# In-place block sums, a second off-diagonal buffer, and norm work moved to GpSimd in a two-layer trunk

## The chip, the cores and the metric

One core of one Trainium2 chip runs the whole kernel in one launch. The metric is device time in microseconds (us), the median of timed runs. PE is TensorE (matmuls), PEld its weight loads, DVE VectorE, ACT ScalarE, POOL GpSimd; SP is the queue that issues most DMAs.

## The reference

Two layers run over 640 tokens: 128 context tokens and 512 latent tokens that share the weights. Each layer is an adaLN-modulated mixer (short conv, windowed attention, gated DeltaNet), an output projection with a gated residual, a second RMS norm with modulation, and a SwiGLU block. What the change touches is the last part, cut to its core:

```python
x  = x + g1 * y                                   # y: mixer output @ w_out
h2 = _rms(x, p['norm2_g']) * (1 + sc2) + sh2      # mean of squares over 1024 features
x  = x + g2 * ((jax.nn.silu(h2 @ p['w_gate']) * (h2 @ p['w_up'])) @ p['w_down'])
```

D_MODEL is 1024, D_FF 2816, everything float32.

## The kernel before

Activations are feature-major: xt[0..7] are tiles of 128 features by 640 tokens. Tokens are worked in two halves h of 320 columns (HB). For accuracy each float32 operand is split into a high part of type fp32r (a cast on ACT) and a low part (a subtraction, on DVE unless another engine is named); a product is three matmuls: high by high, high by low, low by high.

The order in which each engine gets its instructions is fixed at build time by a planner: it takes instructions in program order as their inputs and buffers come free in its own model of the time, and those under tc.high_priority() first. At run time each engine works through its own queue in order. A tile of a pool has a tag and a number of buffers; a new tile of that tag waits until one is free.

After the mixer, rows(LATE_OUT, ...) (line 1570, called at line 1611) computes the output projection. It loads w_out in four pieces of 256 columns (load_w, line 177: DMA to raw, high part line 172, low part line 173). The argument side names the pieces whose split goes to xhi/xlo, in pool fp; the others go to whi/wlo, in pool wp. Pool fp lies where the mixer's pool was, so its tiles can be written only when the mixer's tiles there are done. Products go in the order h, then m (the 128-row block). After each, residual (line 543, DVE) updates xt[m], and Norm.add (line 360) squares it on ACT and adds the square into acc on DVE (line 370), except for the last three m (two in the down projection), whose squares go straight to the sums.

Norm.stats (line 372) sums over features with one-column matmuls (lines 396, 398), raises the mean to the power -0.5 on GpSimd (line 403) and broadcasts the result with matmuls (line 406). PairNorm.half then makes, for each of eight feature blocks k, t1 (line 486, DVE), the value h2 (line 489, ACT) and its split (lines 476 and 477 in block, 172 and 173 in parts). For h = 0 these steps are handed back and interleaved with the products of h = 1; for h = 1 they run after the last product. The blocks of h2 are named b11, b21 (h = 0, feature blocks 0 to 3 and 4 to 7) and b12, b22 (h = 1). derive(j) builds the combinations nt1, t2, nt3, nt4 for each j.

The gate and up products of the first two 128-column blocks are done plainly (lines 1733 to 1735; sets: gate's weights in xhi/xlo, up's in whi/wlo). The others are done in pairs of blocks by class Pair, a seven-product scheme for 2x2 blocks (s1 to s7, 12 matmuls each) in place of eight. A Pair loads the diagonal weight blocks into D (tag raw, three buffers, shared with all other weight loads), the off-diagonal ones into O (tag rawx, one buffer), forms the sums Pa and Pb (tag ps, two buffers; lines 1648, 1651, 1652), and splits D into whi/wlo (d), Pa and Pb into xhi/xlo (a, b) and half of O into ohi/olo (o). Line 1669 copies the first bank negated to the next one (ACT); consume is Swiglu.gate (lines 1712, 1714) or Swiglu.up (line 1720 and a split). Between pairs, down adds chunks of the down projection to xt; at the end of layer 0 these rows feed the next layer's Norm in the same way. In layer 0, the adaLN products of layer 1 (lines 284 to 293) are spread among all of this.

Of the kernel before, what the change touches and what calls it, by code (L numbers as in the profile page):

```python
# [8 lines left out]
F32 = mybir.dt.float32  # L9
F32R = mybir.dt.float32r  # L10
# [39 lines left out]
XEV = 'VVVVVVVAVA'  # L50
LAG, LAST_V = 1, True
LATE_OUT = tuple(range(8))
# [56 lines left out]
def hybrid_trunk_kernel(  # L109
# [234 lines left out]
    class Norm:  # L344
# [15 lines left out]
        def add(self, k, parts=(0, 1)):  # L360

            if self.acc[0] is None or self.acc[1] is None and 1 in parts:
                for h in parts:
                    self.acc[h] = self.fp.tile([128, HH], F32, tag=f"acc{h}", name="acc", bufs=1)
                    A.activation(self.acc[h], self.xt[k][:, HB[h][0]:HB[h][1]], AF.Square)
                return
            for h in parts:
                sq = self.ft(HH, "sq")
                A.activation(sq, self.xt[k][:, HB[h][0]:HB[h][1]], AF.Square)
                V.tensor_tensor(out=self.acc[h], in0=self.acc[h], in1=sq, op=ALU.add)  # L370

# [37 lines left out]
        def half(self, h, k0=0, k1=KT_, later=False):  # L409

            n = HH
            if k0 not in self.a_:
                self.a_[k0] = self.a_fn(k0, k1)
            if self.bc[h] is None:
                with tc.high_priority() if HIS else ExitStack():
                    self.stats(h)
            segs = ((1, slice(0, 128)), (0, slice(128, n))) if h == 0 else ((0, slice(0, n)),)
            rests = []

            def step(i):  # L420
                if i < k1 - k0:
                    rests.append(self.high(k0 + i, h, segs, self.a_[k0][:, i]))
                if i >= LAG:
                    rests[i - LAG]()

            steps = [lambda i=i: step(i) for i in range(k1 - k0 + LAG)]
            if later:
                return steps
            for f in steps:
                f()  # L430
# [29 lines left out]
    class PairNorm(Norm):  # L460
# [18 lines left out]

        def value(self, k, h, dst):  # L480

            b0, b1 = HB[h]
            segs = ((1, slice(0, 128)), (0, slice(128, HH))) if h == 0 else ((0, slice(0, HH)),)
            t1 = self.ft(HH, "t1")
            for g, sl in segs:
                V.scalar_tensor_tensor(out=t1[:, sl], in0=self.xt[k][:, b0:b1][:, sl], scalar=self.a_[0][:, k, g:g + 1],
                                       in1=self.bc[h][:, sl], op0=ALU.mult, op1=ALU.mult)
            for g, sl in segs:
                A.activation(dst[:, sl], t1[:, sl], AF.Identity, bias=self.sh[:, k, g:g + 1])

        def half(self, h, later=False):
            if 0 not in self.a_:
                self.a_[0] = self.a_fn(0, KT_)
            self.stats(h)
            if h == 0:
                def step(i, j):
                    if i == 0:
                        self.first[j] = self.fp.tile([128, 2, HH], F32, tag="act", name="h0", bufs=8)
                    self.value(j + 4 * i, 0, self.first[j][:, i])
                    self.block(j, ("b11", "b21")[i], self.first[j][:, i], apool, G if j % 2 else V)  # L500

                return [lambda i=i, j=j: step(i, j) for i in range(2) for j in range(4)]
            room = [self.fp.tile([128, 3, HH], F32, tag=tag, name="h1", bufs=n) for tag, n in (("rawx", 1), ("ps", 2), ("ps", 2))]
            self.second = [room[(k + 1) // 3][:, (k + 1) % 3] for k in range(KT_)]
            for i in range(2):
                for j in range(4):
                    v = self.second[2 * j + i]
                    self.value(j + 4 * i, 1, v)
                    if i:
                        self.block(j, "b22", v, apool)  # L510
                    elif j < 2:
                        self.parts(j, "b12", v, *(self.fp.tile([128, HH], F32R, tag=tag, name=tag, bufs=2) for tag in ("ohi", "olo")))
                    else:
                        self.parts(j, "b12", v, *(self.fp.tile([128, HH], F32R, tag="tp", name="b12", bufs=TP_BUFS) for _ in range(2)))

        def parts(self, j, name, src, hi, lo):
            split(src, hi, lo)
            self.out[j][name] = (hi, lo)
# [1033 lines left out]
    for l in range(depth):  # L1552
# [5 lines left out]
        with tc.tile_pool(name=f"f{l + 1}", bufs=1, reuse_waits="tile") as fp:  # L1558
            last_layer = l == depth - 1
            fp.tile([128, 2, 4, 128], F32, tag="ps", name="ps", bufs=2)  # L1560
            fp.tile([128, 2, 4, 128], F32, tag="rawx", name="rawx", bufs=1)
            xt = [fp.tile([128, TOK], F32, name=f"xt{k}") for k in range(KT_)]
# [46 lines left out]
            for m in range(KT_):  # L1609
                nc.scalar.dma_start(out=xt[m], in_=xscr[m])  # L1610
            rows(LATE_OUT, w_out[l], 2, 4, mix[2:6], mods[l][:, 16:24], norm, side=(0, 1))
            seven = norm
# [12 lines left out]
            class Pair:  # L1625
# [8 lines left out]
                def __init__(self, w, f, consume):  # L1634
                    self.consume = consume
                    c0, c1 = f * 128, (f + 1) * 128
                    D = wp.tile([128, 2, 4, 128], F32, tag="raw", name="rawd", bufs=RAW_BUFS)
                    O = fp.tile([128, 2, 4, 128], F32, tag="rawx", name="rawo", bufs=1)
                    for dst, k0, c in ((D[:, 0], 0, c0), (D[:, 1], 4, c1), (O[:, 1], 0, c1), (O[:, 0], 4, c0)):
                        loads.append(nc.sync.dma_start(out=dst, in_=wslice(w, k0, 4, c, 128)))  # L1640
                    Pa, Pb = (fp.tile([128, 2, 4, 128], F32, tag="ps", name=name, bufs=2) for name in ("pa", "pb"))
                    self.d = [wp.tile([128, 2, 4, 128], F32R, tag=tag, name=tag, bufs=W_BUFS) for tag in ("whi", "wlo")]
# [3 lines left out]
                    with tc.high_priority():  # L1646
# [52 lines left out]
                def s7(self):  # L1699
                    self.product(Z, self.of(self.b, 1), "b22", False)  # L1700
                    self.consume(Z, 0, 1)

            class Swiglu:
# [12 lines left out]
                def up(self, src, i, h):  # L1716
# [113 lines left out]
```

## Time and profile before

| | |
|---|---|
| timed runs | 1804.47, 1806.52, 1807.45 us; median 1806.52 |
| profiled execution | 1814.66 us, span 1812.6 us |
| PE busy | 1701.5 us, 94% of the span |
| DVE busy | 1247.3 us, 69% |
| ACT busy | 782.1 us, 43% |
| POOL busy | 127.8 us, 7% |
| granted TensorE clock, mean | 0.965 |
| HBM traffic | 103 GB/s over the span |

Busy times count an engine's instructions, not its waits. The granted clock is in parts of full speed. Idle time of an engine matters only where the engine that sets the end waits for it. Layer 0's output projection starts near 417 us, its pairs run from about 495 to 900 us; layer 1's projection starts near 1304 us, its pairs run from about 1382 us to near the end.

### The profile page before, as it was taken

What the parts mean: (1) busy time and instruction counts of PE and PEld (TensorE: products, weight loads), DVE (VectorE), ACT (ScalarE), POOL (GpSimd) and SP (SyncE); (2) the same over time, 40 slices, a digit from 0 to 9 for tenths busy, and PEclk for the clock granted to TensorE, in tenths of its full rate; (3) what the DMA queues carried; (4) which work ended last, traced back from release to release, by engine and by line L of the source; (5) the groups of instructions that cost most, each with busy time, mean ns of one, the idle gap of its engine ahead of it and who ended that gap; (6) DMA issues with size and microseconds to landing.
All of it is one profiled execution on the core that took longest, in us unless ns stands there. A gap on an engine that the chain in (4) does not pass through costs nothing. (4 is left out here: it accounts for less than half of the span.)

```text
span 1812.6 us, 34382 instructions
## 1 busy us (share of the span) xinstructions
PE 1701.5 (94%) x13789; PEld 1512.9 (83%) x13789; DVE 1247.3 (69%) x2778; ACT 782.1 (43%) x1620; POOL 127.8 (7%) x242
## 2 busy tenths in 40 slices
PE   6998999999999999999999899899998999999998
PEld 3887875478889999999997889555897999999998
DVE  3799667665766767666677995686558766667664
ACT  3554234544543433433455532455345342534332
POOL 1110112100200000000012001120011000000000
PEclk7998998999999999999999989899989999999999
DMA  9512233654444222222131221445622322122312
GB/s 302 157 48 68 81 97 114 201 163 143 129 132 124 81 83 86 78 82 82 60 122 48 65 78 56 135 140 161 224 68 59 93 82 82 59 82 71 101 63 59
DMA packets 207693, 188.42 MB, mean 104 GB/s; under 512 B 12782, under 2 KB 182702, under 8 KB 207534
## 3 DMA queue, kind: packets, MB, share of 16 engines
q1 hardware_dynamic: 190656, 170.71, 30.8%
q10 hardware_dynamic: 16878, 15.53, 2.7%
q8 instruction: 108, 1.77, 0.4%
q14 instruction: 51, 0.42, 0.1%
HBM read 168.64 MB, written 17.56 MB: 103 GB/s over the span
## 5 line engine op out<-in xcount | busy, mean ns | idle before, releaser
L172 ACT CAST whi<-raw 128x1024 fp32r<-128x1024 f32 (+1 forms) x102 | 99.9, 980 | 111.7 <-PE pmm L201 34.9
L173 DVE TENSOR_TENSOR wlo<-raw,whi 128x1024 fp32r<-128x1024 f32 (+1 forms) x102 | 116.0, 1138 | 31.8 <-ACT whi L172 31.0
L202 PE MATMUL pmm<-hh,wlo 128*128 128x320 f32 x336 | 109.8, 328 | 6.2 <-DVE wlo L173 6.1
L199 PE MATMUL pmm<-hh,whi 128*128 128x320 f32 x336 | 110.2, 329 | 5.3 <-ACT dnp L614 3.7
L201 PE MATMUL pmm<-hl,whi 128*128 128x320 f32 x320 | 103.7, 324 | 0.0
L199 PE MATMUL pmx<-acth,whi 128*128 128x320 f32 x320 | 100.0, 313 | 3.9 <-DVE xt L543 3.8
L199 PE MATMUL pmm<-acth,whi 128*128 128x320 f32 x320 | 100.2, 313 | 1.4 <-DVE xt L543 1.4
L201 PE MATMUL pmx<-actl,whi 128*128 128x320 f32 x320 | 99.6, 311 | 0.0
L202 PE MATMUL pmx<-acth,wlo 128*128 128x320 f32 x320 | 99.4, 311 | 0.0
L202 PE MATMUL pmm<-acth,wlo 128*128 128x320 f32 x320 | 99.2, 310 | 0.0
L201 PE MATMUL pmm<-actl,whi 128*128 128x320 f32 x320 | 99.0, 309 | 0.0
L543 DVE SCALAR_TENSOR_TENSOR xt<-pmx,mod,xt 128x128 f32<-128x128 f32 (+2 forms) x168 | 68.9, 434 | 39.9 <-PE pmx L202 37.9
L543 DVE SCALAR_TENSOR_TENSOR xt<-pmm,mod,xt 128x128 f32<-128x128 f32 (+2 forms) x168 | 68.3, 432 | 29.4 <-PE pmm L202 18.7
L172 ACT CAST whi<-rawd 128x1024 fp32r<-128x1024 f32 x40 | 41.9, 1049 | 105.6 <-PE pmx L201 62.9
L173 DVE TENSOR_TENSOR xlo<-pb,xhi 128x1024 fp32r<-128x1024 f32 x40 | 49.0, 1225 | 38.0 <-ACT xhi L172 37.2
L199 PEld LDWEIGHTS pmm<-hh,whi 128*128 128x128 f32 x336 | 66.7, 199 | 7.5 <-ACT dnp L614 4.6
L202 PEld LDWEIGHTS pmm<-hh,wlo 128*128 128x128 f32 x336 | 66.3, 197 | 7.9 <-DVE wlo L173 7.0
L286 PE MATMUL pdn<-adaw,c 128*32 128x256 f32 x640 | 63.2, 395 | 9.3 <-DMA adaw<-in_ada_w_dram 9.3
L589 PE MATMUL pmm<-wlo,hh 128*128 128x256 f32 x240 | 69.2, 288 | 0.4 <-DVE wlo L173 0.4
L588 PE MATMUL pmm<-whi,hh 128*128 128x256 f32 x240 | 69.4, 290 | 0.0
L590 PE MATMUL pmm<-whi,hl 128*128 128x256 f32 x240 | 69.3, 289 | 0.0
L1648 DVE TENSOR_TENSOR pa<-rawd,rawo 128x1024 f32<-128x1024 f32 x40 | 50.2, 1255 | 25.4 <-DMA rawo<-in_w_gate_dram 13.4
(558 smaller groups left out, 5623.2 us busy)
## 6 DMA issues: line engine op xcount, KB each, us to landing
adaw<-in_ada_w_dram SPq DMA_DIRECT2D x80, 512.0 KB, 3.9
raw<-in_w_down_dram SPq DMA_DIRECT2D x44, 512.0 KB, 3.5
raw<-in_w_in_dram SPq DMA_DIRECT2D x36, 512.0 KB, 4.6
rawd<-in_w_gate_dram SPq DMA_DIRECT2D x40, 256.0 KB, 3.5
rawo<-in_w_gate_dram SPq DMA_DIRECT2D x40, 256.0 KB, 4.6
rawd<-in_w_up_dram SPq DMA_DIRECT2D x40, 256.0 KB, 3.4
rawo<-in_w_up_dram SPq DMA_DIRECT2D x40, 256.0 KB, 3.7
araw<-in_ada_w_dram SPq DMA_DIRECT2D x16, 512.0 KB, 5.7
```

Source lines behind the costliest of these rows:

```text
L172: (hi_eng or A.copy)(hi, src)
L173: (lo_eng or V).tensor_tensor(out=lo, in0=src, in1=hi.bitcast(F32), op=ALU.subtract)
L199: mm(o, lhsT=wh[:, k], rhs=ah, start=k == 0, stop=False)
L201: mm(o, lhsT=wh[:, k], rhs=al, start=False, stop=False)
L202: mm(o, lhsT=wl[:, k], rhs=ah, start=False, stop=not lead and k == n - 1)
L286: mm(pr[32 * q:32 * q + 32, 0:256], lhsT=c32[:, k], rhs=raw[:, q * 256:(q + 1) * 256], start=k == 0, stop=k == 7)
L543: V.scalar_tensor_tensor(out=x[:, sl], in0=pt[:, a0:a1], scalar=gate[:, g:g + 1], in1=x[:, sl], op0=ALU.mult, op1=ALU.add)
L588: mm(pt, lhsT=ah[:, ts], rhs=wh[:, k % 4], start=k == 0, stop=False)
L589: mm(pt, lhsT=ah[:, ts], rhs=wl[:, k % 4], start=False, stop=False)
L590: mm(pt, lhsT=al[:, ts], rhs=wh[:, k % 4], start=False, stop=k == 7)
L1648: V.tensor_tensor(out=flat(Pa), in0=flat(D), in1=flat(O)[:, 1:2].to_broadcast([128, 2, 512]), op=ALU.add)
```

## The change

- O (rawx) gets two buffers, ps one. The sums formerly in Pb are written over O: its second half becomes Pa[1] + D[0] and its first half O[0] + that sum. The two halves of b change places in s4 and s7.
- PairNorm's values are staged: t1 for step n is issued together with the value and split of step n - 2. The plain Norm keeps its lag of 1.
- For h = 1, PairNorm's stats runs under high priority.
- The adds of squares go to GpSimd, and so do the low parts of b12 for odd j.
- In the output projection the first two weight pieces go to whi/wlo and the last two to xhi/xlo, the other way round from before; the gate and up sets change places in the same way.
- The values of h = 1 lie in two rawx tiles and one ps tile instead of one and two.

```diff
-LAG, LAST_V = 1, True
+LAG, LAST_V = 2, True
...
-                V.tensor_tensor(out=self.acc[h], in0=self.acc[h], in1=sq, op=ALU.add)
+                G.tensor_tensor(out=self.acc[h], in0=self.acc[h], in1=sq, op=ALU.add)
...
-                if i >= LAG:
-                    rests[i - LAG]()
+                if i >= 1:
+                    rests[i - 1]()
...
+        def staged(self, h, order, rest):
+            ts = {}
+            def step(n):
+                if n < len(order):
+                    i, j = order[n]
+                    ts[n] = self.scaled(j + 4 * i, h)
+                if n >= LAG:
+                    i, j = order[n - LAG]
+                    rest(i, j, ts.pop(n - LAG))
+            return [lambda n=n: step(n) for n in range(len(order) + LAG)]
...
-            self.stats(h)
+            with tc.high_priority() if h else ExitStack():
+                self.stats(h)
...
-            room = [self.fp.tile([128, 3, HH], F32, tag=tag, name="h1", bufs=n) for tag, n in (("rawx", 1), ("ps", 2), ("ps", 2))]
+            room = [self.fp.tile([128, 3, HH], F32, tag=tag, name="h1", bufs=n) for tag, n in (("rawx", 2), ("ps", 1), ("rawx", 2))]
...
-            split(src, hi, lo)
+            split(src, hi, lo, lo_eng=G if j % 2 else V)
...
-            rows(LATE_OUT, w_out[l], 2, 4, mix[2:6], mods[l][:, 16:24], norm, side=(0, 1))
+            rows(LATE_OUT, w_out[l], 2, 4, mix[2:6], mods[l][:, 16:24], norm, side=(2, 3))
...
-                    O = fp.tile([128, 2, 4, 128], F32, tag="rawx", name="rawo", bufs=1)
+                    O = fp.tile([128, 2, 4, 128], F32, tag="rawx", name="rawo", bufs=2)
...
-                    Pa, Pb = (fp.tile([128, 2, 4, 128], F32, tag="ps", name=name, bufs=2) for name in ("pa", "pb"))
+                    Pa = fp.tile([128, 2, 4, 128], F32, tag="ps", name="pa", bufs=1)
...
-                        V.tensor_tensor(out=Pb[:, 0], in0=Pa[:, 1], in1=D[:, 0], op=ALU.add)
-                        V.tensor_tensor(out=Pb[:, 1], in0=Pb[:, 0], in1=O[:, 0], op=ALU.add)
-                        split(flat(Pb), flat(self.b[0]), flat(self.b[1]))
+                        V.tensor_tensor(out=O[:, 1], in0=Pa[:, 1], in1=D[:, 0], op=ALU.add)
+                        V.tensor_tensor(out=O[:, 0], in0=O[:, 0], in1=O[:, 1], op=ALU.add)
+                        split(flat(O), flat(self.b[0]), flat(self.b[1]))
...
-                    self.product(Y, self.of(self.b, 0), "t2", False)
+                    self.product(Y, self.of(self.b, 1), "t2", False)
...
-                    self.product(Z, self.of(self.b, 1), "b22", False)
+                    self.product(Z, self.of(self.b, 0), "b22", False)
...
-                    for w, use, side in ((w_gate, sw.gate, fp), (w_up, sw.up, None)) for i in range(2)]
+                    for w, use, side in ((w_gate, sw.gate, None), (w_up, sw.up, fp)) for i in range(2)]
```

## Rows read from the trace of the kernel before

**Rows 1.** Windows: stretch, length, busy (count) of PE, PEld, DVE, ACT, POOL, then PEclk.

```profile
440.00:530.00 90.00, 85.13 (x592) 75.49 (x592) 68.04 (x122) 48.49 (x103) 13.61 (x13) 0.96 0.43 130
530.00:900.00 370.00, 365.50 (x2458) 356.07 (x2457) 250.47 (x424) 145.88 (x241) 0.00 (x0) 1.00 0.29 86
1345.00:1420.00 75.00, 65.19 (x420) 61.84 (x419) 55.99 (x97) 38.88 (x83) 11.12 (x11) 0.95 0.21 64
1420.00:1760.00 340.00, 335.65 (x2241) 328.42 (x2240) 231.73 (x386) 132.51 (x217) 0.00 (x0) 1.00 0.26 78
```

**Rows 2.** TensorE's waits, 1345 to 1420 us: total us, times, longest.

```profile
PE pmm L1659 <- DVE av L1720: 2.8, 1, 2.8
PE pmm L1733 <- DVE sg L1714: 2.6, 1, 2.6
PE pkq L1659 <- ACT xhi L172: 1.2, 1, 1.2
...
PE pmm L1661 <- DVE wlo L173: 0.7, 1, 0.7
PE pkq L1745 <- DVE t L486: 0.6, 1, 0.6
```

**Rows 3.** Timeline of one pair's loads and split, layer 0: start, us, instruction.

```profile
668.61 1.23 DVE L173 TENSOR_TENSOR xlo<-pb,xhi 128x1024 fp32r<-128x1024 f32 x1 [0.45 <-ACT xhi L172]
...
670.87 0.69 DVE L1652 TENSOR_TENSOR pb<-pb,rawo 128x512 f32<-128x512 f32 x1
...
671.59 0.92 SPq L1640 DMA_DIRECT2D rawo<-in_w_gate_dram  x2
...
676.89 0.62 ACT L172 CAST ohi<-rawo 128x512 fp32r<-128x512 f32 x1 [1.04 <-DMA rawo<-in_w_gate_dram]
...
678.26 0.41 PE L1659 MATMUL pkq<-b,xhi 128*128 128x320 f32 x1 [0.86 <-ACT pkq L1669]
```

**Rows 4.** TensorE's waits over the whole span, one row.

```profile
PE pkq L1659 <- ACT pkq L1669: 4.9, 7, 1.3
```

**Rows 5.** Windows, second half of the second norm in layer 1.

```profile
1347.60:1354.60 7.00, 6.22 (x60) 5.95 (x59) 0.20 (x2) 1.24 (x4) 1.89 (x2) 1.00 0.01 2
1354.60:1365.50 10.90, 7.79 (x41) 7.29 (x40) 8.45 (x18) 8.03 (x19) 2.03 (x2) 0.83 0.00 0
1365.50:1390.20 24.70, 22.68 (x141) 22.07 (x142) 23.77 (x39) 12.33 (x25) 6.32 (x6) 0.94 0.22 64
```

**Rows 6.** Timeline, VectorE and TensorE, 1345 to 1354 us.

```profile
1345.72 0.55 DVE L543 SCALAR_TENSOR_TENSOR xt<-pmx,mod,xt 128x320 f32<-128x320 f32 x1
...
1353.45 1.12 PE L406 MATMUL pkq<-ident,ny 80*128 80x80 f32 x8 [0.78 <-POOL ny L403]
```

**Rows 7.** TensorE's waits, 500 to 530 us, layer 0.

```profile
PE pkq L1659 <- ACT pkq L1669: 1.2, 2, 0.8
PE pmx L1660 <- DVE nt L477: 1.0, 1, 1.0
```

**Rows 8.** Timeline, GpSimd and VectorE, 1335 to 1341 us.

```profile
1335.42 1.56 POOL L477 TENSOR_TENSOR b<-h,b 128x320 fp32r<-128x320 f32 x1 [10.57 <-ACT b L476]
...
1336.15 1.17 DVE L370 TENSOR_TENSOR acc<-acc,sq 128x320 f32<-128x320 f32 x1
...
1340.88 0.88 POOL L477 TENSOR_TENSOR b<-h,b 128x320 fp32r<-128x320 f32 x1 [3.91 <-ACT b L476]
```

**Rows 9.** Line 370 as a group: count, shortest, median and longest in ns.

```profile
L370 DVE TENSOR_TENSOR acc<-acc,sq x26: 477/483/1170, 429.8 to 1341.7; 128x320 f32<-128x320 f32 x26
```

**Rows 10.** Timeline, from the mixer into the output projection, layer 1.

```profile
1299.45 1.05 ACT L172 CAST whi<-raw 128x1024 fp32r<-128x1024 f32 x1 [2.83 <-DMA raw<-in_w_out_dram]
...
1301.03 0.65 PE L1392 MATMUL pmx<-pp,VS 128*64 128x256 f32 x4 [1.05 <-ACT pp L1390]
...
1302.79 1.05 ACT L172 CAST xhi<-raw 128x1024 fp32r<-128x1024 f32 x1
...
1312.90 0.68 DVE L543 SCALAR_TENSOR_TENSOR xt<-pmm,mod,xt 128x128 f32<-128x128 f32 x2 [3.16 <-DMA xt<-xscr]
```

More of the change, by code (lines that the diff above doesn't have):

```diff
@@ L422, in step @@
                     rests.append(self.high(k0 + i, h, segs, self.a_[k0][:, i]))
-                if i >= LAG:
-                    rests[i - LAG]()
-            steps = [lambda i=i: step(i) for i in range(k1 - k0 + LAG)]
+                if i >= 1:
+                    rests[i - 1]()
+            steps = [lambda i=i: step(i) for i in range(k1 - k0 + 1)]
             if later:
@@ L478, in block, with scaled, segs, value @@
             self.out[j][name] = (b[:, 0], b[:, 1])
-        def value(self, k, h, dst):
+        def scaled(self, k, h):
             b0, b1 = HB[h]
-            segs = ((1, slice(0, 128)), (0, slice(128, HH))) if h == 0 else ((0, slice(0, HH)),)
             t1 = self.ft(HH, "t1")
-            for g, sl in segs:
+            for g, sl in self.segs(h):
                 V.scalar_tensor_tensor(out=t1[:, sl], in0=self.xt[k][:, b0:b1][:, sl], scalar=self.a_[0][:, k, g:g + 1],
                                        in1=self.bc[h][:, sl], op0=ALU.mult, op1=ALU.mult)
-            for g, sl in segs:
-                A.activation(dst[:, sl], t1[:, sl], AF.Identity, bias=self.sh[:, k, g:g + 1])
+            return t1
+        def segs(self, h):
+            return ((1, slice(0, 128)), (0, slice(128, HH))) if h == 0 else ((0, slice(0, HH)),)
+        def value(self, k, h, t1, dst):
+            for g, sl in self.segs(h):
+                A.activation(dst[:, sl], t1[:, sl], AF.Identity, bias=self.sh[:, k, g:g + 1])
+        def staged(self, h, order, rest):
[8 more added lines that the diff above has]
+            return [lambda n=n: step(n) for n in range(len(order) + LAG)]
         def half(self, h, later=False):
@@ L493, in half, with rest @@
                 self.a_[0] = self.a_fn(0, KT_)
-            self.stats(h)
+            with tc.high_priority() if h else ExitStack():
+                self.stats(h)
+            order = [(i, j) for i in range(2) for j in range(4)]
             if h == 0:
-                def step(i, j):
+                def rest(i, j, t1):
                     if i == 0:
                         self.first[j] = self.fp.tile([128, 2, HH], F32, tag="act", name="h0", bufs=8)
-                    self.value(j + 4 * i, 0, self.first[j][:, i])
+                    self.value(j + 4 * i, 0, t1, self.first[j][:, i])
@@ L500, in step @@
                     self.block(j, ("b11", "b21")[i], self.first[j][:, i], apool, G if j % 2 else V)
-                return [lambda i=i, j=j: step(i, j) for i in range(2) for j in range(4)]
-            room = [self.fp.tile([128, 3, HH], F32, tag=tag, name="h1", bufs=n) for tag, n in (("rawx", 1), ("ps", 2), ("ps", 2))]
+                return self.staged(0, order, rest)
+            room = [self.fp.tile([128, 3, HH], F32, tag=tag, name="h1", bufs=n) for tag, n in (("rawx", 2), ("ps", 1), ("rawx", 2))]
@@ L504, in half, with rest @@
             self.second = [room[(k + 1) // 3][:, (k + 1) % 3] for k in range(KT_)]
[L505 to L514, printed above, removed]
+            def rest(i, j, t1):
+                v = self.second[2 * j + i]
+                self.value(j + 4 * i, 1, t1, v)
+                if i:
+                    self.block(j, "b22", v, apool)
+                elif j < 2:
+                    self.parts(j, "b12", v, *(self.fp.tile([128, HH], F32R, tag=tag, name=tag, bufs=2) for tag in ("ohi", "olo")))
+                else:
+                    self.parts(j, "b12", v, *(self.fp.tile([128, HH], F32R, tag="tp", name="b12", bufs=TP_BUFS) for _ in range(2)))
@@ L516, in parts @@
+            for f in self.staged(1, order, rest):
+                f()
         def parts(self, j, name, src, hi, lo):
-            split(src, hi, lo)
+            split(src, hi, lo, lo_eng=G if j % 2 else V)
             self.out[j][name] = (hi, lo)
@@ L1559, in hybrid_trunk_kernel @@
             last_layer = l == depth - 1
-            fp.tile([128, 2, 4, 128], F32, tag="ps", name="ps", bufs=2)
-            fp.tile([128, 2, 4, 128], F32, tag="rawx", name="rawx", bufs=1)
+            fp.tile([128, 2, 4, 128], F32, tag="ps", name="ps", bufs=1)
+            fp.tile([128, 2, 4, 128], F32, tag="rawx", name="rawx", bufs=2)
             xt = [fp.tile([128, TOK], F32, name=f"xt{k}") for k in range(KT_)]
```

## The prediction

> **What bounds the kernel now.** The first part of the page says which engine to follow: TensorE is busy for 94% of the span, VectorE for 69%, GpSimd hardly. No edit takes a matmul away, so the change can only win stretches in which TensorE waits or runs at the lower of its two clock levels. I then cut the span into the stages that the diff touches and read length minus PE busy in each [rows 1]. The two stretches of pairs, 530 to 900 and 1420 to 1760 us, leave 4.5 and 4.4 us of 710 at full clock: TensorE-bound, little to win. The stretch from the second norm to the first pairs leaves 4.9 us of 90 in layer 0 and 9.8 us of 75 in layer 1, where the granted clock is 0.95 as well. The waits of that stretch in layer 1 [rows 2] name VectorE first: 2.8 us for av, 2.6 us for sg. These two instructions are short; they are late because VectorE is busy 23.77 of the 24.7 us from 1365.5 on [rows 5]. So that stage is bound by the work queued on VectorE behind the norm's second half, and there most of the gain must come from.
>
> In the pairs I looked for the one wait that has to do with the off-diagonal loads, and followed it backwards [rows 3]: TensorE waits 0.86 us at 678.26 for the negated copy that ScalarE makes of the first bank; ScalarE was late because ohi, ahead of it in the same queue, sat 1.04 us until rawo landed; rawo was issued at 671.59, right behind line 1652 (670.87 to 671.56), the last reader of the one rawx buffer. All waits of that kind sum to 4.9 us in 7 places [rows 4], 1.2 us of it at 500 to 530 us [rows 7].
>
> **The change part by part.**
>
> *Sums in place, two rawx buffers.* Instruction count and shapes on every engine stay: line 1651 writes into O instead of Pb, line 1652 over O. The loads are the same four per pair. What moves is the release: before, the next O waits for line 1652; after, O is held until its sum is split (the xlo of b), but there is a second one, so the next load waits for the split of the pair before. In the trace that split ends at 668.61 + 1.23 = 669.84 and line 1652 at 671.56: the load gets only 1.7 us earlier, not a whole pair [rows 3]. That is more than the 1.04 us that ScalarE sat here, and the 1.3 us of the longest such wait [rows 4]. Outside 500 to 530 us there are 4.9 - 1.2 = 3.7 us to win; I take 2.5, because the load stands in SP's queue behind w_down's loads, which still wait for the raw buffers. Bounds 0 and 3.7. The single ps buffer costs nothing: Pa of the next pair is written on VectorE after the last reader of this one, on the same engine.
>
> *The norm's second half earlier and staged (layer 1).* Before, the last residual of the output projection runs on VectorE at 1345.72 to 1346.27, behind norm steps and square sums, and the broadcast of its statistics starts only at 1353.45 [rows 6]; from 1347.6 to 1354.6 VectorE does 0.20 us of work and ScalarE 1.24 [rows 5]. With priority the three late squares, the column sums on TensorE and the power on GpSimd come first: I estimate 3 of these 7 us saved. Then 1354.6 to 1365.5: VectorE busy 8.45 and ScalarE 8.03 of 10.9 us, so each waits for the other for 2.5 to 2.9 us; issuing the scaling two steps ahead takes most of that out, an estimate of 2 us. Together sg comes some 5 us sooner, more than the 2.6 us that TensorE waited for it. What goes with it: 2.6 + 0.6 us of waits [rows 2], and the low clock behind the gap, (1 - 0.94) x 24.7 = 1.5 us at the granted clock of 1365.5 to 1390.2 [rows 5]. Sum 4.7; bounds 0 and 4.7.
>
> *First pairs of layer 1.* They wait for 2.8 + 1.2 + 0.7 = 4.7 us [rows 2]. Late next is VectorE itself: TensorE now also arrives some 4.7 us sooner, while VectorE's queue starts 5 us sooner and has some idle taken out. The exchange of weight buffers lets the first pair's diagonal be split as soon as the gate's products end, not the up's. I take 3.0, bounds 0 and 4.7.
>
> *The same in layer 0.* There the adaLN products of the next layer fill TensorE, and sg costs it next to nothing. At 500 to 530 us it waits 1.2 us for the negated copy and 1.0 us for a low part of nt [rows 7]. I take 1.8, bounds 0 and 2.2.
>
> *Square sums and low parts on GpSimd.* 26 adds leave VectorE at 0.48 us each [rows 9], 12.5 us in all; two lows per layer (odd j) take 4 more. On GpSimd such an operation takes 0.88 us alone and 1.56 us where it meets VectorE; the add at 1336.15 took 1.17 us instead of 0.48 beside one [rows 8]. So a moved add frees 0.48 and, where it meets a two-input operation, costs up to 0.69. Between +0.48 and -0.21 us each, I take half: 26 x 0.13 = 3.5 us of VectorE time freed, all of it beside TensorE's work, and already inside the earlier residual above. The new cost is in GpSimd's queue: the power that every statistic needs can stand behind one add or one low. Bounds per statistic 0 and 1.56 us; on six statistics 0 to 9.4. I take 1.0 in all, since the trace shows GpSimd busy for some 2 us in stretches of 7 and 10.9 us here [rows 5].
>
> The Trainium skill (SBUF — State Buffer, Who interferes with whom) speaks against this part: a VectorE instruction with two SBUF inputs and a GpSimd instruction that reads SBUF lock each other out for the whole instruction. The pair at 1335.42 and 1336.15 agrees; the median of 483 ns beside a maximum of 1170 [rows 9] says that most of these adds met nobody. By the rule taken at its worst, all 30 moved operations would block VectorE for 0.88 us, 26 us against 14 freed.
>
> *Exchange of buffers at the output projection.* Before, its first weights go into xhi, which overlays the mixer's tiles: the split comes at 1302.79, while the weights for the later columns were split at 1299.45 into whi; TensorE meanwhile waited 1.05 us inside the attention's tail [rows 10]. After, the first products can fill such gaps. But the residual that frees the bank waits for xt, 3.16 us at 1312.90 [rows 10], and xt isn't moved: what TensorE wins in front it may stand for behind. I take 1.0 per layer, bounds 0 and 2.0, together 2.0.
>
> **Sum.** 2.5 + 4.7 + 3.0 + 1.8 + 2.0 - 1.0 = 13.0 us. The profiled execution's own time is 1814.66 us (span 1812.6 and 2.1 around it), which would become 1801.7. The median of the timed runs is 1806.52, 8.1 us below the profiled one; the same 13.0 off it gives 1793.5 us. The ends: all bounds won, 3.7 + 4.7 + 4.7 + 2.2 + 4.0 = 19.3, and some idle that I can't name, 3 us: 1784. Nothing won and the queue at its worst: 1816.
>
> **The rivals.**
>
> *Covered.* VectorE is the bound of the stage, and what the norm gains is spent in the weight splits behind it; in the output projection xt decides. Only the O loads and a little remain: -2.5 - 1.0 + 0.5, 1803.5 us. For it: 23.77 of 24.7 us busy. Against it: the 2.5 to 2.9 us of mutual waiting in front.
>
> *GpSimd's queue decides: slower.* Adds and lows stand ahead of the power at 1.56 us each, six times, 9.4 us, with TensorE standing directly for it (it already waits 0.78 us for the power at 1353.45 [rows 6]); the four b12 lows come 1.56 - 0.48 = 1.1 us later each on the chain of the second half, 4.3 us. The norm's gain is gone; O loads and buffers keep 4.5: +9.2, 1815.7 us. It decides from where GpSimd's queue holds the power longer than the 3 us that priority gains. The lock rule cited above would drive it. Against it: GpSimd is idle most of these stages.
>
> *All of it.* Every listed stall goes: 1784 to 1787 us.
>
> *The change doesn't do what it says.* SP's queue keeps O behind w_down's loads, and the second buffer changes nothing: 1793.5 + 2.5 = 1796 us.
>
> **How the numbers follow.** Forecast 0.46, covered 0.21, slower 0.15, all 0.13, O unchanged 0.05. A change under 0.2% (3.6 us) can't be told from none here. Faster: 0.46 + 0.13 + 0.05 and a third of covered, 0.71. Same: the rest of covered and a little of the slower case, 0.16. Slower 0.13. The range 1784 to 1808 leaves out most of the slower case and the far end of the best. For the forecast alone it is 1789 to 1799.
>
> **What would show it.** Right: between the two norm halves of layer 1 VectorE's gap shrinks from 7 to about 4 us; the wait of line 1733's first matmul for sg is gone, and the first pair follows some 5 us sooner; ohi's waits for rawo shrink, and TensorE's waits for the negated copy fall below 2 us; output-projection matmuls stand between the last attention products. Wrong: the power starts late behind an add on GpSimd, the stretch 1345 to 1420 keeps its length, or new waits for xt stand in the projection. Anything that moves the mixers by more than a few us would have a cause that I haven't named.

## The result, and the profile after

The changed kernel takes 1784.54 us (median of 4 runs, 1783.57 to 1785.53) against 1805.49 us for the kernel before (4 runs, too): ratio 0.989, 95% interval [0.9865, 0.9915]. That is 21 us faster; 13 were forecast. The profiled executions took 1783.57 us (span 1781.6) and 1814.66 us. The kernel before, profiled once more, took 1801.69, so 31 us between the first two profiles overstates the change.

Below the norm every line stands 25 lower now (L543 is L568, L1659 is L1684, L1669 is L1694, L1714 is L1739, L1720 is L1745, L1733 is L1758), in the experiments 24 to 27. The busy times over the span after:

```profile
span 1781.6 us, 34378 instructions
PE 1685.3 (95%) x13789; PEld 1506.5 (85%) x13789; DVE 1233.8 (69%) x2748; ACT 782.3 (44%) x1620; POOL 160.1 (9%) x272
```

Span less PE busy is TensorE's idle time: 96.3 us, before 1812.6 - 1701.5 = 111.1. The same by stage: I cut the span at the last attention product, the last broadcast of the norm's statistics, the first and the last pair, and the first product of layer 1. Windows of the kernel before, columns as in [rows 1]: output projection, second norm and pairs of layer 1, and, last, the end of layer 0 (down products and the next norm).

```profile
1303.20:1354.30 51.10, 47.97 (x333) 46.04 (x329) 27.59 (x62) 21.71 (x48) 6.22 (x6) 0.93 0.40 124
1354.30:1381.20 26.90, 23.69 (x141) 23.19 (x141) 24.15 (x43) 16.39 (x37) 8.35 (x8) 0.87 0.07 20
1381.20:1776.00 394.80, 384.79 (x2556) 374.71 (x2556) 270.06 (x448) 157.82 (x262) 0.00 (x0) 1.00 0.26 78
893.50:945.90 52.40, 50.34 (x343) 48.98 (x342) 37.70 (x87) 26.82 (x58) 8.53 (x15) 0.93 0.31 100
```

The same four of the kernel after:

```profile
1280.40:1328.00 47.60, 42.94 (x297) 41.01 (x294) 24.11 (x54) 21.90 (x48) 15.12 (x14) 0.93 0.39 123
1328.00:1352.80 24.80, 24.80 (x161) 24.80 (x161) 23.62 (x39) 15.78 (x36) 11.53 (x10) 0.93 0.08 22
1352.80:1745.00 392.20, 386.13 (x2556) 377.84 (x2556) 270.48 (x451) 158.38 (x265) 0.00 (x0) 0.99 0.26 79
881.10:932.70 51.60, 50.33 (x343) 49.13 (x343) 33.62 (x77) 26.90 (x59) 17.84 (x25) 0.93 0.31 99
```

Three things are to be seen in layer 1. The projection's window holds 36 matmuls fewer (333 to 297), an effect of the exchanged weight buffers to a large part: 16 stand ahead of it now, inside the attention's tail (the mixer in front has 3399, before 3383), and 20 behind the last broadcast (141 to 161). VectorE has 8 instructions fewer there, and 10 fewer at the end of layer 0; GpSimd has them (6 to 14, 15 to 25): the adds of squares. And the norm stage has no idle time left (3.2 us before), while the projection has more (3.1 to 4.7). With both profiles of each kernel, idle time in us:

| stage | before, twice | after, twice | mean change |
|---|---|---|---|
| two mixers | 77.6, 79.6 | 72.0, 70.4 | -7.4 |
| two output projections | 5.3, 4.4 | 8.9, 8.5 | +3.8 |
| two second norms | 3.5, 3.0 | 0.0, 0.0 | -3.2 |
| two stretches of pairs | 18.2, 15.1 | 9.6, 11.1 | -6.3 |
| end of layer 0 | 2.1, 2.2 | 1.3, 1.3 | -0.9 |
| tail | 4.6, 4.6 | 4.5, 4.6 | 0.0 |
| whole span | 111.1, 108.8 | 96.3, 95.8 | -13.9 |

Half of the fall is in the mixers, where only the exchange of buffers moves instructions. Since the matmuls that the exchange moves to the front fill idle time there and are missing in the projection, the two rows belong together: 83.4 to 79.9 us, or -3.6. The norms and the pairs fell by 9.5.

The rest of the 21 us is the busy time of the same 13789 matmuls: 1701.5 and 1691.1 before, 1685.3 and 1684.4 after.

TensorE's waits in the kernel after, 1350 to 1745 us, answer to [rows 2]:

```profile
PE pkq L1684 <- ACT pkq L1694: 2.8, 1, 2.8
PE pmm L199 <- DVE xt L568: 2.7, 1, 2.7
PE pkq L1684 <- ACT u L1710: 0.2, 1, 0.2
PE pmm L1686 <- DVE wlo L173: 0.2, 1, 0.2
```

The waits for av and sg are gone. The two at the top are new in size (in the first profile before, the longest of their kinds are 1.3 and 1.1 us); the second stands once in layer 0 as well, 2.7 us at 830.87. Ahead of this stretch, 1270 to 1365 us, the kernel after waits in other places, too:

```profile
PE pkq L406 <- POOL ny L403: 1.6, 2, 0.8
PE pmm L199 <- DVE xt L568: 1.4, 1, 1.4
PE pxo L396 <- POOL acc L370: 1.2, 1, 1.2
```

The second half of the norm in layer 1, timeline and windows of the kernel after, answers to [rows 5, 6]:

```profile
1321.23 0.54 DVE L568 SCALAR_TENSOR_TENSOR xt<-pmx,mod,xt 128x320 f32<-128x320 f32 x1
1321.70 1.19 ACT L391 ACTIVATE sq<-xt 128x320 f32<-128x320 f32 x3
...
1325.89 0.16 DVE L401 TENSOR_SCALAR nms<-pxo 80x4 f32<-80x4 f32 x1 [3.14 <-PE pxo L398]
1326.13 1.02 POOL L403 TENSOR_TENSOR ny<-nms,mhalf 80x4 f32<-80x4 f32 x1 [4.08 <-DVE nms L401]
...
1327.20 1.12 PE L406 MATMUL pkq<-ident,ny 80*128 80x80 f32 x8 [0.79 <-POOL ny L403]
1328.41 0.55 DVE L485 SCALAR_TENSOR_TENSOR t<-xt,msc,pkq 128x320 f32<-128x320 f32 x1 [2.36 <-PE pkq L406]
```

```profile
1321.70:1328.40 6.70, 5.91 (x57) 5.64 (x56) 1.21 (x5) 2.29 (x7) 2.20 (x3) 0.99 0.27 78
1328.40:1352.80 24.40, 24.40 (x158) 24.40 (x157) 23.62 (x39) 15.78 (x36) 11.53 (x10) 0.93 0.08 23
```

From the last residual to the broadcast it is 5.97 us (1321.23 to 1327.20), before 7.73 (1345.72 to 1353.45): 1.8 us sooner. Behind it VectorE is busy for 23.62 of 24.4 us, and TensorE never stands.

### The profile page after: what moved, and what is told of

The parts are those of the page before. It is cut to its first block, busy times and chain, and to the rows that moved or that the text cites. A ratio compares the mean times of both kernels' runs of the same rounds, so it can differ in the third digit from the quotient of the medians.

```text
span 1781.6 us, 34378 instructions
## 1 busy us (share of the span) xinstructions
PE 1685.3 (95%) x13789; PEld 1506.5 (85%) x13789; DVE 1233.8 (69%) x2748; ACT 782.3 (44%) x1620; POOL 160.1 (9%) x272
## 5 line engine op out<-in xcount | busy, mean ns | idle before, releaser
L568 DVE SCALAR_TENSOR_TENSOR xt<-pmx,mod,xt 128x128 f32<-128x128 f32 (+2 forms) x168 | 69.0, 434 | 50.2 <-PE pmx L202 47.9
L202 PE MATMUL pmx<-acth,wlo 128*128 128x320 f32 x320 | 99.8, 312 | 0.0
L201 PE MATMUL pmm<-actl,whi 128*128 128x320 f32 x320 | 99.8, 312 | 0.0
L568 DVE SCALAR_TENSOR_TENSOR xt<-pmm,mod,xt 128x128 f32<-128x128 f32 (+2 forms) x168 | 68.4, 433 | 38.1 <-PE pmm L202 25.8
L370 POOL TENSOR_TENSOR acc<-acc,sq 128x320 f32<-128x320 f32 x26 | 28.6, 1101 | 615.9 <-ACT sq L369 615.4
L173 DVE TENSOR_TENSOR xlo<-rawo,xhi 128x1024 fp32r<-128x1024 f32 x40 | 49.0, 1225 | 27.4 <-ACT xhi L172 26.5
```

The lines of the kernel that those rows point to most:

```text
L173: (lo_eng or V).tensor_tensor(out=lo, in0=src, in1=hi.bitcast(F32), op=ALU.subtract)
L201: mm(o, lhsT=wh[:, k], rhs=al, start=False, stop=False)
L202: mm(o, lhsT=wl[:, k], rhs=ah, start=False, stop=not lead and k == n - 1)
L568: V.scalar_tensor_tensor(out=x[:, sl], in0=pt[:, a0:a1], scalar=gate[:, g:g + 1], in1=x[:, sl], op0=ALU.mult, op1=ALU.add)
```

## The experiments

All ratios are to the kernel before. Idle time is span less PE busy of one profile. The two repeats set what either can tell: 2.3 and 0.5 us of idle time, and a few per mille of the timed runs. The last column but one is the idle time outside the mixers, to be set against 33.6 us in the first profile before and 24.3 in the first after; it varies by 4.3 and 1.1 us between the repeats. It leaves out the mixers, where only the exchange moves instructions, and so it serves to compare kernels that have the same weight buffers.

| kernel | timed us | ratio, 95% interval | idle | outside the mixers | PE busy |
|---|---|---|---|---|---|
| e1, without the O buffers | 1786.03 | 0.9909 [0.9879, 0.9938] | 96.6 | 27.1 | 1686.6 |
| e2, without the exchange | 1789.04 | 0.9924 [0.9896, 0.9953] | 95.5 | 22.0 | 1689.0 |
| e3, without GpSimd's part | 1794.42 | 0.9944 [0.9924, 0.9964] | 101.8 | 30.0 | 1685.5 |
| e4, without staging and priority | 1790.57 | 0.992 [0.9904, 0.9936] | 101.1 | 29.2 | 1689.7 |
| e5, before again | 1806.53 | 0.9986 [0.9961, 1.0011] | 108.8 | 29.2 | 1691.1 |
| e6, after again | 1786.11 | 0.988 [0.984, 0.9921] | 95.8 | 25.4 | 1684.4 |
| e7, GpSimd's part alone | 1794.54 | 0.9941 [0.9906, 0.9976] | 103.3 | 26.2 | 1687.7 |
| e8, staging and priority alone | 1797.28 | 0.9936 [0.9911, 0.996] | 107.4 | 25.0 | 1695.7 |
| e9, adds back on VectorE | 1797.7 | 0.9942 [0.9918, 0.9966] | 99.8 | 27.4 | 1691.5 |
| e10, O buffers alone | 1805.81 | 1.0003 [0.9974, 1.0031] | 109.3 | 30.0 | 1698.0 |
| e11, residuals and negated copies first | 1782.31 | 0.9859 [0.983, 0.9889] | 92.8 | 19.1 | 1688.3 |
| e12, gates' small steps first, too | 1781.62 | 0.9879 [0.9846, 0.9912] | 97.1 | 20.3 | 1682.7 |

### One part undone

**e1**, the sums and buffers of the pairs as before:

```diff
-                    O = fp.tile([128, 2, 4, 128], F32, tag="rawx", name="rawo", bufs=2)
+                    O = fp.tile([128, 2, 4, 128], F32, tag="rawx", name="rawo", bufs=1)
...
-                        V.tensor_tensor(out=O[:, 1], in0=Pa[:, 1], in1=D[:, 0], op=ALU.add)
+                        V.tensor_tensor(out=Pb[:, 0], in0=Pa[:, 1], in1=D[:, 0], op=ALU.add)
```

> The changed kernel with one rawx buffer, two ps buffers and Pb again; all else as changed. Theory A (the norm's second half and the first pairs behind it carry the gain, the O loads 2.5 us): about 1787.5 us, with 1805.5 for before and 1784.5 for the changed kernel. Theory B (the pairs carry it: O loads come early enough to take ScalarE's waits away everywhere): 1790 us or more, and TensorE's waits for the negated copy back near 4.9 us.

Timed, nothing can be told from the changed kernel, which speaks against theory B; B's sign, the waits for the negated copy, came back all the same. The waits over the whole span of e1 say why that costs little:

```profile
PE pkq L1684 <- ACT pkq L1694: 6.6, 7, 1.6
PE pmm L199 <- DVE xt L568: 3.6, 6, 1.3
```

The waits for negated copies are back, but the two of 2.7 us for xt in the down products are gone. e10 shows the other side.

**e2**, the weight buffers of the projection as before:

```diff
-            rows(LATE_OUT, w_out[l], 2, 4, mix[2:6], mods[l][:, 16:24], norm, side=(2, 3))
+            rows(LATE_OUT, w_out[l], 2, 4, mix[2:6], mods[l][:, 16:24], norm, side=(0, 1))
...
-                    for w, use, side in ((w_gate, sw.gate, None), (w_up, sw.up, fp)) for i in range(2)]
+                    for w, use, side in ((w_gate, sw.gate, fp), (w_up, sw.up, None)) for i in range(2)]
```

> The changed kernel with the buffer sides of the output projection and of the gate and up sets as before. Theory A: the gaps in the attention's tail come back, 2 us in all, 1786.5 us. Rival (the loads of xt decide, so what TensorE wins in front it waits for behind): 1784.5 us within 1. If the side also decides when the first pair can start: 1790 us.

Against the mean of the two profiles after, idle time grows by 2.3 us in the mixers (71.2 to 73.5) and shrinks by 2.9 in the projections (8.7 to 5.8): what TensorE wins in front it stands for behind, as the rival says. Timed it is 0.0034 slower than the changed kernel, nearer to the 1790 us of the last theory, but the intervals overlap; unclear.

**e3**, adds and low parts back on VectorE:

```diff
-                G.tensor_tensor(out=self.acc[h], in0=self.acc[h], in1=sq, op=ALU.add)
+                V.tensor_tensor(out=self.acc[h], in0=self.acc[h], in1=sq, op=ALU.add)
...
-            split(src, hi, lo, lo_eng=G if j % 2 else V)
+            split(src, hi, lo)
```

> The changed kernel with the adds of squares and the low parts of b12 back on VectorE. Theory A: VectorE's relief lies beside TensorE and GpSimd's queue costs about 1 us: 1783.5 to 1785.5 us. Rival 1 (GpSimd's queue holds the statistics): undoing it wins, 1780 us or less. Rival 2 (the freed VectorE time is what brings the second half forward): 1788 us or more.

Rival 2 holds, 1788 or more: ratio 0.9944 [0.9924, 0.9964], the only one of the four above the changed kernel's interval; idle time +5.7. Its interval overlaps with that of e4, so which of these two parts is worth more is not told by undoing them. TensorE's waits of e3, 1350 to 1745 us, show some of it: av and xhi (and sg, 0.3 us) stand ahead of the first pairs again.

```profile
PE pkq L1684 <- ACT pkq L1694: 3.0, 1, 3.0
PE pmm L199 <- DVE xt L568: 2.7, 1, 2.7
PE pmm L1684 <- DVE av L1745: 1.5, 1, 1.5
PE pmx L1684 <- ACT xhi L172: 0.7, 1, 0.7
```

The end of layer 0 in e3, the window to set against the fourth row after, has its 10 adds and nearly 1 us of idle time back (2.22 against 1.27):

```profile
883.50:936.70 53.20, 50.98 (x343) 48.99 (x342) 37.33 (x87) 26.84 (x58) 8.55 (x15) 0.94 0.30 97
```

In every profile with the adds on VectorE this idle time is 2.1 to 2.3 us; with the adds on GpSimd it is 1.3 (1.8 in e11 and e12, which order the residuals otherwise).

**e4**, lag and priority as before (the lag of 1 that the change replaces was the plain Norm's; PairNorm had none):

```diff
-LAG, LAST_V = 2, True
+LAG, LAST_V = 0, True
...
-            with tc.high_priority() if h else ExitStack():
-                self.stats(h)
+            self.stats(h)
```

> The changed kernel without the lag of 2 in PairNorm and without the priority of the second statistics. Theory A: the wait of line 1758 (1733 before) for sg and the low clock behind it come back and the first pairs start late again: 1792 to 1794 us. Theory B (the pairs carry the gain): 1788 us or less.

Between the theories: idle time +5.1, ratio 0.992, its interval overlaps with the changed kernel's. The gate's wait for sg comes back with 0.5 us only, not 2.6 [rows 2], so GpSimd's part goes a long way to take it away alone; in layer 0 the first pair waits 1.5 us for av.

### Repeats, and parts alone

**e5** and **e6** are the two kernels again, without an edit.

> The kernel before, unchanged, for a second profile. Both theories: the stages that the change touches (both projections to the next mixer) take the same 1038.7 us within 1.5, since their instruction order is fixed. If the mixers (416.6 and 357.3 us in the first profile) are as long again, the changed kernel's shorter mixers (409.9 and 347.7 us with the same order of matmuls) are an effect of the change; if they fall to about 411 and 350 us, the first profile was a long execution and the change didn't touch them.

> The changed kernel, unchanged, for a second profile: 1784.5 us within 5, its touched stages 1024.0 us within 1.5. This is the yardstick for what a difference between two profiles is worth.

The repeats agree less well than expected: the touched stages take 1035.4 us in e5 and 1020.0 in e6, 3.3 and 4.0 less than in the first profiles. The mixers take 414.6 and 349.9 us in e5, so the first was no shorter to speak of and the second 7.4: the first profile was a long one there, and mixer lengths of two single profiles don't show an effect of the change. Much of such a difference is the clock. The end of layer 0 in e6, against the fourth row after:

```profile
887.20:935.70 48.50, 47.25 (x344) 46.04 (x343) 33.55 (x77) 26.81 (x59) 17.81 (x25) 1.00 0.33 106
```

Same kernel, same matmuls, 1.25 against 1.27 us of idle time: 3.1 us shorter at a granted clock of 1.00 instead of 0.93. This is why I went over to idle time.

**e7** is the kernel before with e3's lines in their new form, **e8** the kernel before with e4's, made from the changed kernel by undoing the rest:

```diff
 # e7: undone beside e1 and e2
-LAG, LAST_V = 2, True
+LAG, LAST_V = 0, True
...
 # e8: undone beside e1 and e2
-                G.tensor_tensor(out=self.acc[h], in0=self.acc[h], in1=sq, op=ALU.add)
+                V.tensor_tensor(out=self.acc[h], in0=self.acc[h], in1=sq, op=ALU.add)
```

> The kernel before with only the adds of squares and the b12 lows moved to GpSimd. After the runs that undid one part, theory C: the time that this frees on VectorE is what brings the second half of the norm forward, so it wins much by itself, touched stages 1031 us or less, 1796 us. Theory A (prediction): nothing or 1 us lost, 1804 to 1806 us.

> The kernel before with only the staging by two steps and the priority of the second statistics. Theory A: 9.5 us won, 1796 us, touched stages 1029 us. Theory C (VectorE's queue still holds the last residuals and so the squares, whatever their priority): 3 us or less won, touched stages 1036 us or more.

Timed both are near 0.994, some 11 us each: theory C in e7 and theory A in e8, whose touched stages, 1028.5 and 1031.5 us, lie on the same side. By the whole idle time GpSimd's part alone takes 6.7 us off (mean before 110.0) and staging 2.6, but that difference is no effect of the parts. It is all in the first mixer, where neither edit touches a line; e7, then e8:

```profile
0.00:413.90 413.90, 366.05 (x3667) 284.76 (x3667) 288.10 (x809) 190.84 (x457) 49.04 (x111) 0.94 0.44 138
0.00:418.20 418.20, 366.10 (x3665) 285.61 (x3667) 287.80 (x809) 190.38 (x457) 49.01 (x111) 0.93 0.43 136
```

That is 47.9 against 52.1 us of idle time. Outside the mixers staging takes 6.4 off the mean before of 31.4, GpSimd's part 5.2: the two parts can't be told apart in size. They differ in what they end. e7 still waits 0.9 us for sg and 2.7 for av in layer 1, e8 for neither. And from the last residual of layer 1's projection to the broadcast it is 7.70 us in e7 (1324.48 to 1332.18) and in e4 (1325.73 to 1333.43), as before the change, but 6.16 in e8 (1339.41 to 1345.57) and 6.15 in e3 (1327.37 to 1333.52): this chain is shorter where the statistics have priority, and GpSimd's adds make no difference to it.

### Which half of GpSimd's part, and the O buffers alone

**e9**, only the adds back on VectorE:

```diff
-                G.tensor_tensor(out=self.acc[h], in0=self.acc[h], in1=sq, op=ALU.add)
+                V.tensor_tensor(out=self.acc[h], in0=self.acc[h], in1=sq, op=ALU.add)
```

> The changed kernel with the 26 adds of the squares back on VectorE; the low parts of second-half blocks stay on GpSimd (two of four per layer). Undoing both together cost about 8 us of the touched stages (1032.4 against 1024.0 and 1020.0) and came to 1794.4 timed. Theory 'adds': the 26 adds hold nearly all of it, since they are what VectorE had between the residuals that the attention projection's last products wait for: 1792 to 1795, touched stages 1028 to 1032, attention-to-gate stages of both layers 4 us longer each, and the wait of the statistics (L396) for acc goes. Theory 'lows': the few low parts lie right between the second half's values and the first pairs, and they hold most: 1784 to 1788, touched stages about 1022. My own first reading, that GpSimd's queue costs 1 us: 1783 to 1785, with the 1.17 us waits at the statistics gone in both layers.

Theory "adds": 0.9942 like e3, idle time +3.8 of its +5.7. The four lows are left with the difference, 1.9, no more than a repeat varies. The sign that this theory named, an end of the wait for acc, did not come: the statistics' first products wait in either kernel. Whole span, e9 and then the kernel after:

```profile
PE pxo L396 <- DVE acc L370: 4.4, 5, 1.6
```

```profile
PE pxo L396 <- POOL acc L370: 2.3, 2, 1.2
```

On VectorE an add takes half as long and still is awaited longer. In e9's timeline its square is ready on ScalarE by 1319.07, and it stands behind a weight split:

```profile
1318.25 0.82 ACT L369 ACTIVATE sq<-xt 128x320 f32<-128x320 f32 x2
1318.38 1.23 DVE L173 TENSOR_TENSOR wlo<-raw,whi 128x1024 fp32r<-128x1024 f32 x1 [0.21 <-ACT whi L172]
1319.52 0.49 DVE L370 TENSOR_TENSOR acc<-acc,sq 128x320 f32<-128x320 f32 x1
```

**e10**, the kernel before with the O buffers alone (e2, e3 and e4 undone together):

```diff
-LAG, LAST_V = 2, True
+LAG, LAST_V = 0, True
...
-            split(src, hi, lo, lo_eng=G if j % 2 else V)
+            split(src, hi, lo)
```

> The kernel before with only the two buffers for off-diagonal loads and the sums in place. Theory 'separate': the buffers are worth what undoing them cost, 1.8 us of touched stages, near the 2.5 us forecast: 1801 to 1805 beside a before of about 1805, touched stages 1034 to 1036 against 1037. Theory 'needs the rest': the off-diagonal halves matter only when the second half no longer sets the start of the first pairs, so alone they give nothing: 1805 +- 1.5, and ohi's wait for rawo shrinks without the first pair starting earlier. Theory 'steady pairs': the two buffers also help pairs outside the first: pairs0 and pairs1 each at least 2 us shorter than 397.7 and 393.8.

Theory "needs the rest" has the number: 1.0003 [0.9974, 1.0031], idle time -0.7, touched stages 1036.9 us; the steady pairs got no 2 us shorter each (400.1 and 393.3). But the reason is another than that theory's. Its waits for negated copies are gone (4.9 us in 7 places before, 2.9 in 6 in e5), and this row of the whole span is there instead:

```profile
PE pmm L199 <- DVE xt L567: 5.6, 3, 2.7
```

Two waits of 2.7 us for xt stand in every kernel with the second rawx buffer but e11 and e12, and in none without. The kernel after at the first of them:

```profile
828.18 0.34 DVE L568 SCALAR_TENSOR_TENSOR xt<-pmm,mod,xt 128x128 f32<-128x128 f32 x1
828.44 0.68 DVE L1677 TENSOR_TENSOR rawo<-rawo 128x512 f32<-128x512 f32 x1
829.16 1.23 DVE L173 TENSOR_TENSOR xlo<-rawo,xhi 128x1024 fp32r<-128x1024 f32 x1
830.31 0.41 DVE L568 SCALAR_TENSOR_TENSOR xt<-pmm,mod,xt 128x192 f32<-128x192 f32 x1
...
830.87 0.39 PE L199 MATMUL pmm<-acth,whi 128*128 128x320 f32 x1 [2.67 <-DVE xt L568]
```

A residual is two instructions here. Between them VectorE takes the second sum and its split, which have priority, and TensorE waits for the bank that the residual frees.

### A version that takes the new waits away

In the first pair of layer 1 it is ScalarE's order; the kernel after:

```profile
1355.30 0.68 DVE L1677 TENSOR_TENSOR rawo<-rawo 128x512 f32<-128x512 f32 x1
...
1356.07 1.05 ACT L172 CAST xhi<-rawo 128x1024 fp32r<-128x1024 f32 x1 [2.00 <-DVE rawo L1677]
1357.02 0.42 ACT L1694 ACTIVATE pkq<-pmm 128x320 f32<-128x320 f32 x1
...
1357.49 0.42 PE L1684 MATMUL pkq<-t,xhi 128*128 128x320 f32 x1 [2.82 <-ACT pkq L1694]
```

The negated copy stands behind a split that waited 2.00 us for the in-place sum. **e11** puts residuals and negated copies ahead:

```diff
-                    residual(xt[m], pt, h, gate[:, m])
+                    with tc.high_priority():
+                        residual(xt[m], pt, h, gate[:, m])
...
-                    A.activation(Y, self.x, AF.Copy, scale=-1.0)
+                    with tc.high_priority():
+                        A.activation(Y, self.x, AF.Copy, scale=-1.0)
```

> The changed kernel with two more steps put ahead in the planner's order: the residual of the projection and of the feed-forward down products, and the negated copy that the first pair's second product adds to. They aim at what the changed kernel's trace now names: TensorE waits for xt in down products 7.4 us over 4, for the negated copies 3.6 us over 2, for xt in the projection 2.1 us over 2. Theory 'waits go': 6 to 10 us less than the changed kernel, 1775 to 1780. Theory 'turned into other waits': what stood ahead on VectorE, the splits of the next weights, is now late instead; TensorE then waits for xlo or wlo about as long, 1783 to 1787. Theory 'worse': weight splits that were hidden become the bound in every chunk of down products, over 1788.

Between "waits go" and "turned into other waits". Both waits of 2.7 us for xt are gone, the negated copy is down to 0.6 us in either layer; what stands there instead, 1350 to 1745 us:

```profile
PE pmx L1685 <- DVE sg L1741: 2.7, 1, 2.7
PE pmm L1687 <- DVE wlo L173: 0.7, 2, 0.5
PE pkq L1685 <- ACT pkq L1696: 0.6, 1, 0.6
```

Idle time 92.8, the lowest here (19.1 outside the mixers against 24.3 and 25.4), ratio 0.9859 [0.983, 0.9889]. It beats the kernel before; against the changed kernel the intervals overlap, and the two were not timed in the same rounds.

**e12** puts the gates' small steps ahead, too:

```diff
-                    use(o, i, h)
+                    with tc.high_priority():
+                        use(o, i, h)
```

> The kernel with residuals and negated copies first, and beside them the gates' own small operations on VectorE and ScalarE (the sg and av steps of the first set of feed-forward products) put ahead in the planner's order, against the 2.7 us for which the first pair of layer 1 waited for sg in that kernel. TensorE's idle time over the span was 96.3 and 95.8 us in the changed kernel, 92.8 with residuals first; the busy time of its 13789 matmuls differs by up to 10 us between profiles of one kernel with the granted clock, so idle time is the measure. Theory 'the wait goes': idle 89.5 to 91, 1778 to 1781 timed. Theory 'it moves again': the splits of the first pair's weights come later and TensorE waits for xhi or xlo instead: idle 92 to 95, 1781 to 1785.

"It moves again". The wait for sg is gone, and 1270 to 1745 us has these, near the first pairs:

```profile
PE pkq L1685 <- ACT pkq L1696: 2.1, 2, 1.5
PE pmx L1686 <- DVE nt L477: 1.8, 1, 1.8
...
PE pmx L1685 <- ACT xhi L172: 0.9, 1, 0.9
```

The whole idle time, 97.1 us, lies above the ranges of both theories, since the mixers, which the edit does not touch, have 76.8 of it. Outside the mixers it is 20.3 us, in e11 19.1, so e12 wins nothing.

## Why the prediction was right and wrong

The direction and the bound (VectorE's queue from the second norm to the first pairs) were right. The time was not well hit: 1784.5 lies half a microsecond inside the lower edge of the stated range, 9 us below the forecast of 1793.5 and outside its 1789 to 1799. It is a time of the rival "all of it", but not by that rival's way: not every listed stall went, and new ones came. Idle time fell by 13.9 us where 13.0 less the 1.5 of clock were forecast. By stage that is near as well: norms and pairs 9.5, forecast (4.7 - 1.5) + 3.0 + 1.8 + 2.5 - 1.0 = 9.5; mixers with projections 3.6, forecast 2.0. By part it is not, so that the sums agree is in part luck: the O buffers gave less than forecast, GpSimd's part more. The step that failed is the term of -1.0, which had the wrong sign.

*GpSimd's part.* I put 26 x 0.13 = 3.5 us of VectorE time down as "beside TensorE's work", and 1.0 us as a loss in GpSimd's queue. Measured, it is a gain as large as the staging's: 5.7 us of idle time when undone, 5.2 alone outside the mixers, some 10 us timed either way. I priced collisions at half of the worst case. VectorE's busy time fell by 1247.3 - 1233.8 = 13.5 us, from e3 to the kernel after by 1245.4 - 1233.8 = 11.6, and the moved operations are worth 26 x 0.483 + 4 x 0.48 = 14.5, so by these sums collisions cost VectorE some 1 to 3 us in all, 0.1 per moved operation at most. The Trainium skill's lock rule (SBUF — State Buffer, Who interferes with whom), which I weighed against this part, agrees with the spread of GpSimd's adds, 868 ns at the least and 1855 at the most, median 880:

```profile
L370 POOL TENSOR_TENSOR acc<-acc,sq x26: 868/880/1855, 418.6 to 1315.1; 128x320 f32<-128x320 f32 x26
```

Its worst case, 26 us, did not come about: 18 of the 26 adds took less than 1 us. And the freed time was not "beside": VectorE had no slack behind the norm ([rows 5], 23.77 of 24.7 us), so the 3.5 us of adds in a projection (VectorE's busy time there, 27.59 to 24.11) can come out of all that is queued behind them. That the gain comes this way is argued; what e7 and e4 show is that it isn't a shorter chain from the last residual to the broadcast (7.70 us in both, 7.73 before). The queue's cost, up to 9.4 us in the slower rival, isn't there. The statistics wait 1.2 us once per layer for acc, 2.3 in all, but this wait is 0.4 us in e7, and with the adds on VectorE and all else as changed it is longer, 4.4 us in e9 and 5.3 in e3. The power's wait stayed (0.78 to 0.79 us at the second half, 5.9 to 5.4 over the span).

*Staging and priority, first pairs, layer 0* (4.7 + 3.0 + 1.8). The mechanism was right: the waits for sg and av are gone. The size is uncertain, 2.6 us of idle time alone (6.4 outside the mixers), undone 5.1; 8.0 were forecast without the clock. GpSimd's part works on the same waits: the gate's for sg, 2.6 us before, is 0.9 us in e7 and 0.5 in e4, and not there at all with staging, alone (e8) or with both. VectorE's gap didn't shrink from 7 to 4 us as I said (6.7 us with 1.21 of work in it, before 7.0 with 0.20 [rows 5]); the chain got 1.8 us shorter, 1.6 of it in e8, and the norm stage 2.5 (two profiles each: 26.9 and 27.2 to 24.8 and 24.3), where I had the first pair 5 us sooner.

*O buffers* (2.5). The waits for the negated copy went as read from [rows 3, 4] in the steady pairs, from 4.9 and 2.9 us to none in e10, and ScalarE's waits of ohi for rawo fell from 49.7 us to 6.5 in the kernel after. But TensorE still waits 3.6 us there for negated copies (4.1 in e6), where I had named less than 2 us as a sign: these waits are in the first pairs now, behind the split of the in-place sum. I had also missed what an earlier load lets loose: its sum and split now arrive in the midst of the down products' residuals, 2 x 2.7 us. Net 0.5 to 0.7 us of idle time, no gain that timing shows. The rival that SP's queue holds the load back is out: those waits did go.

*Exchange of buffers* (2.0). Right in kind, "what TensorE wins in front it may stand for behind": 16 to 18 matmuls per layer moved to the front, and new waits for xt stand in the projections, a thing that I had named as a sign of being wrong. Its net worth isn't settled: by e2's idle time nothing, by its timing 0.0034 with overlapping intervals. Over all fourteen profiles the idle time of mixers and projections together is 78.3 to 82.9 us in the eight with the exchange (mean 80.0) and 79.3 to 86.0 in the six without (mean 83.0): some 3 us, which would account for most of what the mixers lost, with e2 itself, 79.3, not in line. No run has the exchange alone.

*The clock* (1.5, inside the norm's term). Probably too small. Some 7 of the 21 us are left to shorter busy time for the same matmuls, no more than the 10.4 by which the two profiles of the kernel before differ. In the timed runs the mean granted clock is 0.971 after (8 runs) and 0.968 before (70), and a straight line through the runs within each kernel gives some 1.3 us for 0.001 of it, an estimate of 4 us. In the four profiles with over 107 us of idle time PE was busy for 1691 to 1702 us, in the ten with less for 1683 to 1692. No experiment changed the clock alone, so that fewer gaps are the cause is argued, not shown.

## What to carry to other kernels

Where the engine that feeds TensorE has no slack, time taken off it can count even in a stage where TensorE doesn't wait for those instructions: look behind that stage before putting relief down as hidden. A buffer that lets a load come earlier also lets its followers come earlier, with whatever priority they have: ask what they will stand in front of. Two parts that work on the same wait, as both did on the gate's for sg, can't each be credited with all of it. And the total of one profile doesn't rank parts of a 1% change: the first mixer's idle time differed by 4.2 us between two kernels with the same code there.

## What the runs showed of the hardware that was not expected

The end of layer 0 took 51.6 and 48.5 us in two executions of one kernel, with equal idle time, at granted clocks of 0.93 and 1.00, 1.00 being the 2.4 GHz level. Over a whole execution TensorE's busy time differed by 10.4 us between two profiles of the kernel before (1701.5 and 1691.1): half of what this change is worth.
